# Unread products ahead of the two halves of the inverse's merge

## The chip, the cores and the metric

The kernel runs on one core of a Trainium2 chip. A core has a matrix engine (TensorE, PE in the profile), a vector engine (VectorE, DVE), a scalar engine (ScalarE, ACT), GpSimd (POOL) and SyncE (SP), which only issues DMAs. Each engine works through its own list of instructions in order, and waits at an instruction until what it needs from other engines is there. ACT issues DMAs too, and such an issue stands in its list like any other instruction. The metric is the device time of one execution, in microseconds (us).

## The reference, cut to what matters

One layer of a network for 128 prompt tokens and 512 latent tokens. It has a differential attention, a recurrent branch (RWKV7, run forward and backward), and a gated convolution. The change lies in the recurrent branch, which the reference writes as a scan over single tokens:

```python
def rwkv7_scan(s0, r, w, k, v, a, b, reverse):
    ...
    def step(S, inp):
        r_t, w_t, k_t, v_t, a_t, b_t = inp
        sa = jnp.einsum('bhvk,bhk->bhv', S, a_t)
        S = S * w_t[:, :, None, :] + sa[..., None] * b_t[:, :, None, :] + v_t[..., None] * k_t[:, :, None, :]
        return S, jnp.einsum('bhvk,bhk->bhv', S, r_t)
    s_final, ys = lax.scan(step, s0.astype(F32), xs, reverse=reverse)
    return jnp.moveaxis(ys, 0, 1), s_final
...
    q, k, v, rw, gates = jnp.split(proj, ...)      # proj = h @ p['w_in']
```

Eight heads of 64 channels run over 640 tokens in two directions. The other parts of the projection (queries, keys, values, gates) don't depend on the scan.

## The kernel before, in words

The scan is done in chunks of 64 tokens: 10 chunks, 2 directions, 4 pairs of heads. Inside a chunk the steps turn into a triangular system, whose 64x64 matrix must be inverted; between chunks a state of 64x64 is carried on. For each pair of heads i from 0 to 3 the main loop runs these stages:

- `rw_c` makes the triangular matrices of all 40 systems (2 heads, 2 directions, 10 chunks) in the tile MS.
- `rw_i` inverts the two 32x32 blocks on the diagonal of each, step by step on DVE (X, L711 and L713), turns one of them around into Y (L722) and puts the turned results back into MS (L725).
- `rw_m` merges: the block off the diagonal is a product of three 32x32 matrices. The first half (L735) multiplies 40 blocks of MS with Y into a PSUM bank `ps_m`, and ACT copies the result in four pieces to Vt (L737). The second half (L743) multiplies Vt with MS, into the other bank of the two, and DVE and ACT copy four pieces back to MS in turn (L745). Then the starting states are turned and scaled (L755 on PE, L756 on DVE into ST), the operands of the chain are turned (L766 on PE, L770 on ACT into AT), and the chain over the chunks runs: L781 solves, L802 and L805 join, L828 steps.
- `rw_e` and `rw_f` make the outputs, and `rw_b` prepares the next pair of heads (its square kk is L540, its norm rn L517 and L519).

TensorE would have little to do in these chains. So the main loop mixes in the big projections, which need nothing from the scan: `flow` is a generator over them, and `pull(n)` issues the next n products (L215, 128x128 times 128x320). There is a `pull(12)` between the halves of the merge. `pq` (L196) ties every product of this phase to the one before, so that TensorE keeps the order in which the program writes them.

The other engines keep no such order. The tile framework sorts the instructions of DVE, ACT, POOL and SP by its own estimate of when they can run. This matters at the second merge, where the query-key projection of one head ends nearby. There DVE scales a small bias (bs, L246), ACT evicts the product in three pieces to qkt (L956) and issues four DMAs that copy qkt with its 32-row blocks swapped to sw (L961). Then DVE multiplies qkt by the rotary table (L928, L929) while POOL does the same with sw, and DVE adds the two (L964). ACT splits off the high part (qkh, L223).

Of the kernel before, what the change touches and what calls it, by code (L numbers as in the profile page):

```python
# [18 lines left out]
P = 128  # L19
# [9 lines left out]
HALF = T // 2  # L29
# [37 lines left out]
def tile_layer(ctx, tc, x_prompt, x_sample, cache_k, cache_v, state_rwkv, c, c_ctx, w_ada, b_ada, w_in,  # L67
# [4 lines left out]
    nc = tc.nc  # L72
    def chain(prev, bi):
        if prev is not None:
            tc.add_manual_dep(bi.ins, prev.ins.name,
                              mybir.DependencyInfo(mybir.DependencyClass.NoSync, mybir.DependencyReason.DATA),
                              reason="psum group order")
        return bi
# [114 lines left out]
    def pq(bi):  # L193

        if order[0]:
            order[1] = chain(order[1], bi)  # L196
        return bi
# [60 lines left out]
    def bank(pool, tag, bufs=1):  # L258
        return pool.tile([P, 512], F32, name="ps_" + tag, tag=tag, bufs=bufs)
# [13 lines left out]
    xw, xa, xwl, xal = (cb.tile([P, T], F32R, name=n_) for n_ in ("xw", "xa", "xwl", "xal"))  # L273
# [4 lines left out]
    with tc.tile_pool(name="start", bufs=1) as sp, tc.tile_pool(name="psS", bufs=2, space=PSUM) as psS:  # L278
# [61 lines left out]
        for q in range(4):  # L340
# [4 lines left out]
            ps = psS.tile([P, 512], F32, name="ps_ada", tag="ada")  # L345
# [21 lines left out]
        ps, ps2 = (psS.tile([P, 512], F32, name="ps_ada", tag="ada") for _ in range(2))  # L367
# [5 lines left out]
        ps = psS.tile([P, 512], F32, name="ps_ada", tag="ada")  # L373
        prev = None
        for n, (s, w) in enumerate(((shh, wfh), (shh, wfl), (shl, wfh))):
            for kb in range(KB):
                prev = chain(prev, pq(nc.tensor.matmul(ps[0:32, :], s[:, kb, :], w[:, kb].rearrange("p b n -> p (b n)"),
                                                    start=n == 0 and kb == 0, stop=n == 2 and kb == KB - 1)))
        nc.scalar.copy(out=shb[0:32, :], in_=ps[0:32, :])
        ps = psS.tile([P, 512], F32, name="ps_ada", tag="ada")  # L380
# [24 lines left out]
    def token_shift(blk, out, pool, first=None, new=None):  # L405
        rt = raw[nraw[0] % 2]
        nraw[0] += 1

        def evac(cols, pd, bias):
            o = 1 if cols.start == 0 else 3  # L410
            nc.scalar.activation(out=rt[:, o + cols.start:o + cols.stop], in_=pd, func=AF.Identity, bias=bias)

        if first is None:
            yield from project_in(load_w(w_in[:, W_RW + blk * P:W_RW + (blk + 1) * P], KB), evac, new=new)
        elif first > 1:
            ps = firsts[first - 2]
            for v, cols, src in ((0, slice(0, TP), ps[0][:, 0:TP]), (1, slice(TP, HALF), ps[0][:, TP:HALF]), (1, slice(HALF, T), ps[1][:, 0:HALF])):
                evac(cols, src, bias0[:, first, v:v + 1])
        tmp = pool.tile([P, 650], F32, name="shtmp", tag="f", bufs=FB)[:, 0:642]
        nc.scalar.activation(out=tmp, in_=rt[:, 1:643], func=AF.Copy, scale=cmu[:, blk:blk + 1])  # L420
        m0, m1 = vec("mu0", blk), vec("mu1", blk)
        nc.vector.scalar_tensor_tensor(out=tmp, in0=rt[:, 0:642], scalar=m0, in1=tmp, op0=ALU.mult, op1=ALU.add)
        nc.vector.scalar_tensor_tensor(out=out[:, 0:TP], in0=rt[:, 2:130], scalar=m1, in1=tmp[:, 0:128], op0=ALU.mult, op1=ALU.add)
        nc.vector.scalar_tensor_tensor(out=out[:, TP:T], in0=rt[:, 132:644], scalar=m1, in1=tmp[:, 130:642], op0=ALU.mult, op1=ALU.add)
# [4 lines left out]
    def newx():  # L429

        nx[0] += 1
        return (lambda: psD.tile([P, 512], F32, name="ps_d")) if nx[0] % 2 == 0 else lambda: psX.tile([P, 512], F32, name="ps_x", tag="x")
# [8 lines left out]
    def pull(n):  # L441
        for _ in range(n):
            if next(flow[0], None) is None:
                while later:
                    later.pop(0)[1]()
                return False
            for x in later:
                x[0] -= 1
            while later and later[0][0] <= 0:
                later.pop(0)[1]()  # L450
        return True
# [19 lines left out]
    def ft(name, w=T):  # L471
        return rp.tile([P, 650], F32, name=name, tag="f", bufs=FB)[:, 0:w]
# [16 lines left out]

    R = [dict() for _ in range(4)]  # L490

    def rw_a(i):
        cs = slice(i * P, (i + 1) * P)
        upw = ft("upw", 2 * P).rearrange("p (d n) -> p d n", d=2)
        nc.sync.dma_start(out=upw[0:64], in_=rw_w_up[:, :, cs].rearrange("d k n -> k d n"))
        nc.sync.dma_start(out=upw[64:128], in_=rw_a_up[:, :, cs].rearrange("d k n -> k d n"))
        ups_ = rp.tile([P, 2, 2, P], F32R, name="ups", tag="ups", bufs=UPB)
        for z, o in ((0, 0), (1, 64)):
            here, there = slice(o, o + 64), slice(64 - o, 128 - o)
            nc.scalar.copy(out=ups_[here, z], in_=upw[here])  # L500
            nc.gpsimd.tensor_tensor(out=ups_[there, z], in0=upw[here], in1=ups_[here, z].bitcast(F32), op=ALU.subtract)
        r, kr = (rp.tile([P, T], F32, name=n_, tag="rk", bufs=2) for n_ in ("r", "kr"))
        v = rp.tile([P, T], F32, name="v", tag="v", bufs=2)
        R[i].update(r=r, kr=kr, v=v, upw=ups_)
        yield from token_shift(4 + i, kr, rp, 2 if i == 0 else None, None if i == 0 else newx())
        yield from token_shift(i, r, rp, 3 if i == 0 else None, None if i == 0 else newx())
        R[i].update(rk_in=1)
        yield from token_shift(8 + i, v, rp, None, newx())
        R[i].update(v_in=1)
# [218 lines left out]
    def rw_m(i):  # L728
        AR, BT, UV, gs, st_in, MS = (R[i][k] for k in ("AR", "BT", "UV", "gs", "st_in", "MS"))
        Y11 = R[i]["Y11"]  # L730
        Vt = rp.tile([64, 40, 32], F32, name="Vt", tag="bk", bufs=2)
        ps = bank(psR, "m", 2)
        for ix in range(40):
            g, sl = ix % 4, ix // 4
            pq(nc.tensor.matmul(ps[32 * g:32 * g + 32, sl * 32:sl * 32 + 32], MS[0:32, ix, 32:64], Y11[:, :, ix], start=True, stop=True))  # L735
# [2 lines left out]
                out=Vt[32:64, g::4, :], in_=ps[32 * g:32 * g + 32, 0:320].rearrange("p (c s) -> p c s", s=32))  # L738
        pull(12)
        ps = bank(psR, "m", 2)  # L740
        for ix in range(40):
            g, sl = ix % 4, ix // 4
            pq(nc.tensor.matmul(ps[32 * g:32 * g + 32, sl * 32:sl * 32 + 32], Vt[32:64, ix, :], MS[32:64, ix, 32:64], start=True, stop=True))  # L743
# [9 lines left out]
        ps = bank(psR, "m", 2)  # L753
# [250 lines left out]
    def gate(br, n):  # L1004
# [3 lines left out]
        def ev_g(cols, pd, bias):  # L1008
# [6 lines left out]
    vals, heads_, gates = ([lambda z=z: values(z) for z in range(4)], [lambda z=z: qk_head(z) for z in range(4)],  # L1015
                           [lambda z=z: gate(1 - z // 8, z % 8) for z in range(16)])
    pairs_ = [lambda i=i: rw_a(i) for i in range(4)]
    works = [pairs_[0]] + vals[0:3] + [pairs_[1], vals[3]] + heads_[0:2] + [pairs_[2]] + heads_[2:4] + gates[0:1] + [pairs_[3]] + gates[1:]
    flow[0] = (x for f in works for x in f())
# [5 lines left out]
    for i in range(4):  # L1025
        if i:
            rw_e(i - 1)
        else:
            pull(40)
        need(i, "v_in")  # L1030
        sides.append(rw_d(i))
        rw_c(i)
        if i:
            sides.append(rw_f(i - 1))
        rw_i(i)
        if i < 3:
            need(i + 1, "rk_in")
            sides.append(rw_b(i + 1))
        else:
            pull(10)  # L1040
        rw_m(i)
        while sides:
            side()
            pull(3)
# [17 lines left out]
    def abank(tag):  # L1062
        return psA.tile([P, 512], F32, name=tag, tag=tag)
# [14 lines left out]
    ps = abank("T")  # L1078
# [529 lines left out]
```

## Time and profile before

| | us |
|---|---|
| median of the runs shown (3) | 1409.14 |
| lowest and highest | 1409.0 and 1413.62 |
| the profiled execution | 1415.6 |
| its span, first to last instruction | 1413.6 |
| TensorE busy in the span | 1254.3 (89%) |
| DVE busy in the span | 960.7 (68%) |
| ACT busy in the span | 544.0 (38%) |

The profiled execution is one run of its own, and all durations below are from it. A row of the timeline has the start of a group of equal instructions, the time that it took from the first start to the last end, engine, line and operation. In brackets stands how long the engine had been idle, and what released it. The dense products overlap, so their distance and not their length tells the rate. The granted clock is shown as a share of full speed: 1.00 is 2.4 GHz and 0.50 is 1.2 GHz.

### The profile page before, as it was taken

What the parts mean: (1) busy time and instruction counts of PE and PEld (TensorE: products, weight loads), DVE (VectorE), ACT (ScalarE), POOL (GpSimd) and SP (SyncE); (2) the same over time, 40 slices, a digit from 0 to 9 for tenths busy, and PEclk for the clock granted to TensorE, in tenths of its full rate; (3) what the DMA queues carried; (4) which work ended last, traced back from release to release, by engine and by line L of the source; (5) the groups of instructions that cost most, each with busy time, mean ns of one, the idle gap of its engine ahead of it and who ended that gap; (6) DMA issues with size and microseconds to landing.
All of it is one profiled execution on the core that took longest, in us unless ns stands there. A gap on an engine that the chain in (4) does not pass through costs nothing. (4 is left out here: it accounts for less than half of the span.)

```text
span 1413.6 us, 26568 instructions
## 1 busy us (share of the span) xinstructions
PE 1254.3 (89%) x10583; PEld 1118.5 (79%) x10583; DVE 960.7 (68%) x1672; ACT 544.0 (38%) x1122; POOL 553.4 (39%) x415
## 2 busy tenths in 40 slices
PE   6989878887879899999888989969999999999995
PEld 5888777786768788889777777758988988989984
DVE  2367948896868667931366433687997987768778
ACT  3444333333333334232355321464443433434440
POOL 2244225432542232212220244546644635635631
PEclk9989979988998899989889999999999999999998
DMA  9412112221221111212666888423232231322222
GB/s 308 129 41 65 53 58 61 65 75 54 63 72 61 50 34 51 85 50 76 189 183 216 267 259 266 136 72 93 81 106 68 75 97 58 99 69 76 75 75 82
DMA packets 157455, 144.57 MB, mean 102 GB/s; under 512 B 10490, under 2 KB 128020, under 8 KB 157332
## 3 DMA queue, kind: packets, MB, share of 16 engines
q1 hardware_dynamic: 147490, 127.85, 29.6%
q10 hardware_dynamic: 9842, 15.03, 3.1%
q8 instruction: 83, 1.36, 0.4%
q14 instruction: 40, 0.33, 0.1%
HBM read 121.06 MB, written 19.69 MB: 100 GB/s over the span
## 5 line engine op out<-in xcount | busy, mean ns | idle before, releaser
L187 POOL TENSOR_TENSOR wl<-ws,wh 128x512 fp32r<-128x512 f32 x100 | 139.1, 1393 | 393.2 <-ACT wh L186 361.6
L224 POOL TENSOR_TENSOR wl<-sums,wh 128x512 fp32r<-128x512 f32 x88 | 137.0, 1562 | 39.4 <-ACT wh L223 35.7
L1431 PE MATMUL ps_d<-oph,wh 128*128 128x320 f32 x440 | 137.6, 313 | 11.6 <-DVE u L1443 5.2
L224 POOL TENSOR_TENSOR wl<-wu,wh 128x512 fp32r<-128x512 f32 x63 | 88.8, 1409 | 142.6 <-ACT wh L223 129.2
L1431 PE MATMUL ps_d<-oph,wl 128*128 128x320 f32 x440 | 137.0, 311 | 1.2 <-POOL wl L224 1.2
L1431 PE MATMUL ps_d<-opl,wh 128*128 128x320 f32 x440 | 136.5, 310 | 1.1 <-DVE opl L224 1.1
L186 ACT CAST wh<-ws 128x512 fp32r<-128x512 f32 x100 | 61.6, 618 | 136.7 <-PE ps_d L215 37.2
L215 PE MATMUL ps_d<-hh,wl 128*128 128x320 f32 (+1 forms) x304 | 102.8, 338 | 0.0
L215 PE MATMUL ps_x<-hh,wl 128*128 128x320 f32 (+1 forms) x304 | 101.6, 334 | 0.6 <-POOL wl L187 0.6
L215 PE MATMUL ps_d<-hl,wh 128*128 128x320 f32 (+1 forms) x304 | 102.0, 335 | 0.0
L215 PE MATMUL ps_x<-hh,wh 128*128 128x320 f32 (+1 forms) x304 | 101.8, 335 | 0.0
L215 PE MATMUL ps_d<-hh,wh 128*128 128x320 f32 (+1 forms) x304 | 101.6, 334 | 0.0
L215 PE MATMUL ps_x<-hl,wh 128*128 128x320 f32 (+1 forms) x304 | 101.2, 333 | 0.0
L1431 PEld LDWEIGHTS ps_d<-oph,wh 128*128 128x128 f32 x440 | 83.0, 189 | 16.0 <-ACT wh L223 9.1
L1431 PEld LDWEIGHTS ps_d<-opl,wh 128*128 128x128 f32 x440 | 83.0, 189 | 2.3 <-POOL hf L1346 1.3
L1431 PEld LDWEIGHTS ps_d<-oph,wl 128*128 128x128 f32 x440 | 83.1, 189 | 1.9 <-POOL wl L224 1.7
L223 ACT CAST wh<-sums 128x512 fp32r<-128x512 f32 x88 | 54.6, 620 | 64.7 <-PE ps_e L1431 25.2
L1465 PE MATMUL acc<-wh,gh 128*128 128x512 f32 x185 | 73.6, 398 | 2.6 <-ACT gh L223 2.6
L1466 PE MATMUL acc<-wl,gh 128*128 128x512 f32 x185 | 73.4, 397 | 0.0
L1467 PE MATMUL acc<-wh,gl 128*128 128x512 f32 x185 | 72.3, 397 | 0.5 <-DVE gl L224 0.5
L223 ACT CAST wh<-wu 128x512 fp32r<-128x512 f32 x63 | 39.1, 621 | 73.3 <-PE acc L1467 30.1
L215 PEld LDWEIGHTS ps_d<-hh,wl 128*128 128x128 f32 x304 | 61.9, 203 | 2.0
(430 smaller groups left out, 3649.7 us busy)
## 6 DMA issues: line engine op xcount, KB each, us to landing
wu<-in_w_up_dram SPq DMA_DIRECT2D x42, 512.0 KB
ws<-in_w_in_dram SPq DMA_DIRECT2D x76, 256.0 KB
wa<-in_w_ada_dram SPq DMA_DIRECT2D x24, 512.0 KB
ws<-in_w_down_dram SPq DMA_DIRECT2D x44, 256.0 KB
wa<-in_w_ada_dram SPq DMA_DIRECT2D x8, 1024.0 KB
ks<-qk_dram SPq DMA_DIRECT2D x32, 192.0 KB
g_dram<-tg ACTq DMA_DIRECT2D x16, 320.0 KB
tg<-g_dram SPq DMA_DIRECT2D x16, 320.0 KB
```

The costliest lines, as they stand in the source:

```text
L186: nc.scalar.copy(out=wh, in_=ws)
L187: (lo_eng or nc.gpsimd).tensor_tensor(out=wl, in0=ws, in1=wh.bitcast(F32), op=ALU.subtract)
L215: pq(nc.tensor.matmul(pd, w[:, k, :], x[:, g, sl], start=g == 0 and z == 0, stop=g == kb - 1 and z == 2))
L223: nc.scalar.copy(out=hi, in_=src)
L224: (lo_eng or nc.vector).tensor_tensor(out=lo, in0=src, in1=hi.bitcast(F32), op=ALU.subtract)
L1431: nc.tensor.matmul(ps, w[:, k, :], x[:, b, k, :], start=k == 0 and z == 0, stop=k == 3 and z == 2)
L1465: nc.tensor.matmul(acc, a_h, wh, start=first, stop=False)
L1466: nc.tensor.matmul(acc, a_h, wl, start=False, stop=False)
L1467: nc.tensor.matmul(acc, a_l, wh, start=False, stop=last)
```

## The change

A new helper writes n products of 128x128 times 128x320 into the first 320 columns of a given PSUM bank. Their operands are the tile xw, which stays in SBUF through this phase. Nobody reads the result: the products of the merge write the same columns afterwards, with `start=True`. The helper is called in `rw_m` ahead of the first half with 16 products for i = 1 and 2 (none for 0 and 3), and ahead of the second half with 10 products for all four i.

```diff
+    def unread(ps, n):
+
+        for _ in range(n):
+            pq(nc.tensor.matmul(ps[:, 0:HALF], xw[:, 0:P], xw[:, 0:HALF], start=True, stop=True))
...
         ps = bank(psR, "m", 2)
+        unread(ps, 16 if 0 < i < 3 else 0)
         for ix in range(40):
             g, sl = ix % 4, ix // 4
             pq(nc.tensor.matmul(ps[32 * g:32 * g + 32, sl * 32:sl * 32 + 32], MS[0:32, ix, 32:64], Y11[:, :, ix], start=True, stop=True))
...
         pull(12)
         ps = bank(psR, "m", 2)
+        unread(ps, 10)
         for ix in range(40):
```

The new lines shift the later ones: L735 and L737 become L741 and L743, L743 and L745 become L750 and L752, and all behind them (L756, L928, L956, L961, L964) get 7 more. L540 becomes L545.

The framework sorts the other engines' instructions anew around the added products. The first place is TensorE at the second merge (i = 1), from the end of the dense products ahead of it. Before:

```order
L215 MATMUL ps_x<-hl,wh 128x322
L215 MATMUL ps_x<-hh,wl 128x322
L215 MATMUL ps_x<-hh,wh 128x322
L735 MATMUL ps_m<-Y_3266,MS 32x32 x40
L215 MATMUL ps_x<-hl,wh 128x322
```

And now, where L495 is the helper's line:

```order
L215 MATMUL ps_x<-hl,wh 128x322
L215 MATMUL ps_x<-hh,wl 128x322
L215 MATMUL ps_x<-hh,wh 128x322
L495 MATMUL ps_m<-xw 128x320 x16
L741 MATMUL ps_m<-Y_3276,MS 32x32 x40
L215 MATMUL ps_x<-hl,wh 128x322
```

On TensorE nothing else has moved, here or elsewhere: the ten products of the second half stand between its dense products and L750 in the same way.

The second place is ACT at the same merge, from the two conversions of weights (wh) ahead of the Vt copies. Before:

```order
L186 CAST wh<-ws 128x512 x2
L737 COPY Vt<-ps_m 32x10x32 x4
L956 ACTIVATE qkt<-ps_d,bs 128x128
L956 ACTIVATE qkt<-ps_d,bs 128x192
L956 ACTIVATE qkt<-ps_d,bs 128x320
L961 DMA sw<-qkt 32x512 x4
L745 COPY MS<-ps_m 32x10x32
L770 COPY AT<-ps_m 64x512
L186 CAST wh<-ws 128x512
L745 COPY MS<-ps_m 32x10x32
```

And now:

```order
L186 CAST wh<-ws 128x512 x2
L963 ACTIVATE qkt<-ps_d,bs 128x128
L963 ACTIVATE qkt<-ps_d,bs 128x192
L963 ACTIVATE qkt<-ps_d,bs 128x320
L743 COPY Vt<-ps_m 32x10x32
L968 DMA sw<-qkt 32x512 x4
L743 COPY Vt<-ps_m 32x10x32 x3
L752 COPY MS<-ps_m 32x10x32 x2
L223 CAST qkh<-qkt 128x640
L1005 DMA qk_dram<-qkh 128x640
L777 COPY AT<-ps_m 64x512
```

The three evictions to qkt have moved ahead of all Vt copies, and the four DMA issues ahead of three of them. The conversion qkh and its DMA have moved ahead of the first copy to AT.

The third place is DVE at the same merge, from the small bias bs on. Before:

```order
L246 TENSOR_SCALAR bs<-ps_d 128x2
L745 COPY MS<-ps_m 32x10x32
L756 TENSOR_SCALAR ST<-ps_m,gs 128x64 x2
L745 COPY MS<-ps_m 32x10x32
L928 TENSOR_TENSOR qkt<-qkt,rope 128x512
L929 TENSOR_TENSOR qkt<-qkt,rope 128x512
L788 COPY QQ<-ps_ch 64x256
L964 TENSOR_TENSOR qkt<-qkt,sw 128x512
L517 TENSOR_SCALAR rn<-ps_m 128x10
```

And now:

```order
L246 TENSOR_SCALAR bs<-ps_d 128x2
L935 TENSOR_TENSOR qkt<-qkt,rope 128x512
L752 COPY MS<-ps_m 32x10x32
L936 TENSOR_TENSOR qkt<-qkt,rope 128x512
L752 COPY MS<-ps_m 32x10x32
L971 TENSOR_TENSOR qkt<-qkt,sw 128x512
L763 TENSOR_SCALAR ST<-ps_m,gs 128x64 x2
L795 COPY QQ<-ps_ch 64x256
L522 TENSOR_SCALAR rn<-ps_m 128x10
```

The three rotary instructions have moved ahead of the two scalings into ST, and the first of them ahead of the copies into MS. Elsewhere little has moved: at the third merge the square kk (L540) now stands ahead of ACT's four Vt copies instead of behind them, and DVE's bs there comes two instructions later. On POOL, at the second merge, the subtraction of one weight slab (L187) has moved behind the rotary work on sw. On SP two loads have changed places.

## Rows read from the trace of the kernel before

**Rows 1.** The table of waits, TensorE, 160 to 620 us: total, times, longest.

```profile
PE ps_m L743 <- ACT Vt L737: 8.4, 8, 2.4
```

**Rows 2.** Timeline of TensorE, second merge: start, us, instruction, idle time before.

```profile
320.37 0.44 PE L735 MATMUL ps_m<-Y,MS 32*32 32x32 f32 x16 [1.46 <-DVE Y L722]
324.19 1.23 PE L735 MATMUL ps_m<-Y,MS 32*32 32x32 f32 x64 [3.38 <-DVE Y L722]
...
332.25 0.63 PE L766 MATMUL ps_m<-ident,AR 128*64 128x128 f32 x4 [0.38 <-DVE ST L756]
...
341.72 0.33 PE L802 MATMUL ps_m<-BT,QQ 64*64 64x64 f32 x4 [0.65 <-DVE rn L517]
```

**Rows 3.** Timeline of ACT, second merge.

```profile
325.48 1.74 ACT L737 COPY Vt<-ps_m 32x320 f32<-32x320 f32 x4 [6.62 <-PE ps_m L735]
331.00 1.10 ACT L956 ACTIVATE qkt<-ps_d,bs 128x128 f32<-128x128 f32 x3 [3.78 <-DVE bs L246]
332.13 2.59 ACTq L961 DMA_DIRECT2D sw<-qkt  x4
```

**Rows 4.** Timeline of DVE, second merge.

```profile
330.81 0.15 DVE L246 TENSOR_SCALAR bs<-ps_d 128x2 f32<-128x2 f32 x1
330.88 0.47 DVE L745 COPY MS<-ps_m 32x320 f32<-32x320 f32 x1
331.28 0.26 DVE L756 TENSOR_SCALAR ST<-ps_m,gs 128x64 f32<-128x64 f32 x1
...
336.23 0.69 DVE L928 TENSOR_TENSOR qkt<-qkt,rope 128x512 f32<-128x512 f32 x1 [0.53 <-DMA sw<-qkt]
336.95 1.64 DVE L929 TENSOR_TENSOR qkt<-qkt,rope 128x512 f32<-128x512 f32 x1
...
340.89 0.69 DVE L964 TENSOR_TENSOR qkt<-qkt,sw 128x512 f32<-128x512 f32 x1 [1.85 <-POOL sw L929]
```

**Rows 5.** Timeline of TensorE, fourth merge.

```profile
600.10 0.32 PE L215 MATMUL ps_d<-hh,wl 128*128 128x322 f32 x1
600.25 0.31 PE L215 MATMUL ps_d<-hh,wh 128*128 128x322 f32 x1
602.93 2.60 PE L743 MATMUL ps_m<-MS,Vt 32*32 32x32 f32 x80 [2.37 <-ACT Vt L737]
...
607.17 1.06 PE L766 MATMUL ps_m<-ident,AR 128*64 128x128 f32 x4 [0.38 <-DVE ST L756]
...
608.30 0.47 PE L215 MATMUL ps_d<-hh,wl 128*128 128x322 f32 x1
608.56 0.47 PE L215 MATMUL ps_d<-hh,wh 128*128 128x322 f32 x1
```

**Rows 6.** Timeline of TensorE, first merge.

```profile
180.77 0.24 PE L743 MATMUL ps_m<-MS,Vt 32*32 32x32 f32 x2 [2.06 <-ACT Vt L737]
```

**Rows 7.** Timeline of TensorE, third merge.

```profile
479.92 1.27 PE L743 MATMUL ps_m<-MS,Vt 32*32 32x32 f32 x74 [0.20 <-ACT Vt L737]
...
482.70 1.06 PE L766 MATMUL ps_m<-ident,AR 128*64 128x128 f32 x4 [0.38 <-DVE ST L756]
...
491.28 0.33 PE L802 MATMUL ps_m<-BT,QQ 64*64 64x64 f32 x4
```

**Rows 8.** Timeline of POOL, second merge.

```profile
336.38 1.67 POOL L187 TENSOR_TENSOR wl<-ws,wh 128x512 fp32r<-128x512 f32 x1 [16.17 <-ACT wh L186]
338.01 1.49 POOL L928 TENSOR_TENSOR sw<-sw,rope 128x512 f32<-128x512 f32 x1
339.58 1.28 POOL L929 TENSOR_TENSOR sw<-sw,rope 128x512 f32<-128x512 f32 x1
```

**Rows 9.** Timeline of ACT, third merge.

```profile
478.12 1.74 ACT L737 COPY Vt<-ps_m 32x320 f32<-32x320 f32 x4
...
480.46 0.82 ACT L540 ACTIVATE kk<-kr,vT 128x640 f32<-128x640 f32 x1
```

**Rows 10.** Table by stretch: us, busy per engine, granted clock, DMA share, GB/s.

```profile
602.70:612.90 10.20, 8.60 (x122) 7.11 (x124) 1.69 (x5) 4.14 (x10) 1.54 (x2) 0.50 0.27 85
```

## The prediction

> **What bounds the kernel now.** I read the table of waits first, for TensorE in 160 to 620 us, because that stretch holds the four merges. Its longest entry is the merge's second half waiting for the copies of Vt: 8.4 us over eight waits [rows 1]. The view lists ACT, DVE and a little POOL as releasers and no DMA. So in this stretch TensorE and the two vector engines hand work to each other, and a delay of one handover moves all that follows. I call the merges by their order: first near 180 us, second near 325, third near 475, fourth near 600. Then I read the timelines, engine by engine, around the second merge. TensorE stands idle 1.46 us before the first 16 rows of the first half, and 3.38 us before the rest, both times for a DVE transpose [rows 2]. ACT makes four Vt copies as soon as the first half is done, and only then takes up the query-key block: three evictions at 331.00 (1.10 us) and four DMA issues (2.59 us) [rows 3]. DVE is busy without a break up to the small copy bs at 330.81, and bs is what those evictions wait for [rows 4].
>
> **The change part by part.** It adds 72 products of 128x320: 10 in front of the second half in all four merges, 16 in front of the first half in the second and third. It removes nothing. They wait for nothing. One costs 0.15 us, the distance between two such products at full clock, or 0.26 at half clock [rows 5].
>
> *The products themselves.* The 16 take 16 x 0.15 = 2.4 us and start where the idle time starts, at 320.37 - 1.46 = 318.9. They end near 321.3, so the first sixteen small products begin 0.9 us late, but the other 64 wait until 324.19 anyway [rows 2]. Cost 0. The ten take 1.5 us. They fit into 2.06 us of waiting in the first merge [rows 6] and 2.37 in the fourth [rows 5]. Cost 0. If this cover were gone, they would cost 72 x 0.15 = 10.8 us in all.
>
> *The moved instructions, second merge.* The order shows more than an insertion. ACT now has the three evictions and the four DMA issues around the Vt copies: evictions, one copy, four DMA issues, three copies. And DVE has the rotary work of the query block (L928, L929, L964) between the copies into MS and ahead of the two scalings L756 that start the state chain. I follow this with durations of before, on the clock of before:
> - bs ends at 330.96 and the evictions start at 331.00 as now, since nothing ahead of them moves. They end at 332.1 [rows 3, 4].
> - One Vt copy (1.74 / 4 = 0.43) to 332.5. Four DMA issues, 2.59, to 335.1. Three copies, 1.31, to 336.4 [rows 3].
> - The second half needs all four copies. Its last 74 products took 1.27 us at half clock [rows 7], and after such a wait I take that: done at 337.7.
> - DVE: L928 waits for the four transfers. It began at 336.23, which is 1.5 us after the last issue ended (334.72) [rows 3, 4], so now at 336.6. It ends at 337.3, before the products, and costs nothing. The first MS copy (0.47) ends at 338.2 [rows 4].
> - L929 took 1.64 us, and L928 of the same shape 0.69 [rows 4]. Then the second MS copy, 0.48, and L964, 0.69, which also waits for POOL's two multiplications: 336.6 + 1.49 + 1.28 = 339.4 [rows 8]. So L964 ends at 340.1 with the short L929 and at 341.1 with the long one. I take 341.1, because POOL's L929 runs through just that time.
> - L756 begins at 341.2 instead of 331.28, 9.9 us late (8.9 with the short L929) [rows 4].
>
> On L929 the trace and a page can be weighed. Its 1.64 us fell together with a POOL subtraction at 336.38 of 1.67 us [rows 8]. The Trainium skill, "SBUF — State Buffer", section "SBUF: two separate sides", says that VectorE with two operands in SBUF and GpSimd hold their shared ports one at a time, each for its whole instruction. By that rule L929 could stand behind both multiplications of POOL, and L964 would end at 339.4 + 0.69 + 0.48 + 0.69 = 341.3 rather than 341.1. The rows agree in that L929 was long only under a POOL instruction, and the sum would grow by 0.2 us.
>
> Behind L756 wait the second transpose L755, the transposes L766 and with them the whole state chain, since TensorE works in order. Something comes back: from L766 (332.25) to the first L802 (341.72) before took 9.47 us, with 0.65 of waiting at its end for rn, which stood behind L964 [rows 2, 4]. That rotary work is done earlier now. The third merge, where it isn't in the way, takes 482.70 to 491.28 = 8.58 us [rows 7]. So 9.9 - 0.9 = 9.0 us late at L802. Bounds: 8.9 - 0.9 = 8.0, and 9.9 if nothing comes back.
>
> *The moved instruction, third merge.* The square L540 (0.82 us) now stands ahead of the four Vt copies [rows 9]. They begin 0.8 us later. The copies, not the products, are what ends the wait there. Against this stands a possible return of the clock (next term). I take +0.5, bounds +0.8 and -1.2 (0.8 - 2.0).
>
> *The clock.* In the fourth merge the granted clock is 0.50, that is 1.2 GHz, from 602.70 to 612.90 [rows 10], after TensorE had waited from 600.6 to 602.9 [rows 5]. With 1.5 us of that wait filled it may stay at 2.4 GHz. Worth: two groups of transposes L766, 1.06 against 0.63 us each [rows 2, 5], and ten dense products, 10 x (0.26 - 0.15) = 1.1, together 2.0 us. The second half itself gains next to nothing: it is paced by the copies. I take -1.5, bounds 0 and -2.0. First merge: after the ten products TensorE still waits, and what follows the copies hangs on DVE. I take 0, bounds 0 and -2.0.
>
> **Sum.** 0 + 9.0 + 0.5 - 1.5 = +8.0 us. Against its own time, 1415.6 us for the profiled execution (a span of 1413.6 and 2.0 around it), this is 1423.6. The median of the runs shown is 1409.14, 6.5 lower; I carry the difference over: 1409.1 + 8.0 = 1417.1 us. Nothing later takes the delay up, as far as I can see, because DVE and ACT wait with TensorE and what they do next is fed by it.
>
> **The rivals.**
> - *The clock pays most of it back.* The stall costs its 9.0, the square 0.8, but the other three merges each return 2.0: +3.8, 1412.9 us. For it: the clock does fall at these places, and the fill goes just where it is lost. Against: in the first and third merge the wait for the copies ends with more waiting after the fill.
> - *The delay is taken up.* The stretch after the second merge has long DVE work. If that had slack the 9 us would vanish, leaving 0.5 - 1.5 = -1.0, 1408.1 us. For it: TensorE waits for DVE again later. Against: DVE idles through the same stall, so its later work starts later too.
> - *Faster.* The Vt copies keep their time, because the evictions find bs early or the DMA issues pass quickly, and all four merges run at 2.4 GHz from the second half through the second L766: 4 x 2.0 - 0.8 = 7.2 us gained, 1401.9 us. It decides if the copies of the second merge end before 331 us of the old scale. The Trainium skill, "TensorE: Matmul & The Clock Gate", section "Why this matters for your kernels", speaks for this: idle gaps between bursts bring the array back to half clock, so filling them should pay. By that rule alone the time would be the 1401.9 of this rival. The clock in the fourth merge agrees with it; the place of bs on DVE speaks against the rest [rows 4].
> - *The products land on the path.* If the order shifts the waits so that half or more of the 72 have no wait to hide in, 5 to 11 us come on top of the stall: 1422 to 1428 us. Against: each has a wait in front that is longer.
>
> **How the numbers follow.** A difference below 0.5% (7.0 us) can't be told from no change here. Chances: forecast 0.57, with own bounds from 8.0 + 0.5 - 2.0 = +6.5 to 9.9 + 0.8 = +10.7; clock pays back 0.17; taken up 0.12; faster 0.05; on the path 0.09. Four fifths of the forecast's own range lies above 7.0, so slower is 0.57 x 0.8 + 0.09 = 0.55, same 0.11 + 0.17 + 0.12 = 0.40, faster 0.05. The range runs from 1410 (most of the rival in which the clock pays) to 1421 (the forecast's upper bound and a little), and leaves out the faster case, most of "taken up" and most of the last.
>
> **What would show it.** In the second merge: ACT with evictions before the first Vt copy and the four issues before the other three; Vt done some 9 us later than before; TensorE idle twice, before the second half and again before the second L755; L964 ahead of L756 on DVE; the distance from the last transpose Y to the first L802 longer by about 9 us. In the third: L540 before Vt. In the fourth: granted clock 1.00 up to L766 or beyond. I am wrong if the Vt copies of the second merge end less than 5 us later than before, or if that distance grows by less than 6 us.

## The result and the profile after

The changed kernel took 1420.12 us (median of 4 runs, 1419.58 to 1420.44) against 1409.12 for the kernel before (4 runs, 1409.0 to 1413.62). The ratio is 1.0078, with a 95% interval from 1.005 to 1.0107: 11.0 us slower, 7 to 15. The forecast was 1417.1. The profiled execution took 1419.58 with a span of 1417.6; that of before took 1415.6, so these two profiles differ by only 4.0 us.

The table of waits of the changed kernel, TensorE, 160 to 620 us:

```profile
PE ps_m L750 <- ACT Vt L743: 10.3, 14, 2.3
...
PE ps_m L762 <- DVE ST L763: 4.9, 4, 3.0
```

The wait for Vt has grown although ten products now stand in front of it in every merge [rows 1], and a wait for ST with 3.0 us in one piece is new. Both are at the second merge. TensorE there:

```profile
318.03 1.21 PE L741 MATMUL ps_m<-Y,MS 32*32 32x32 f32 x64 [2.71 <-DVE Y L727]
...
326.47 0.24 PE L750 MATMUL ps_m<-MS,Vt 32*32 32x32 f32 x2 [2.25 <-ACT Vt L743]
328.96 2.15 PE L750 MATMUL ps_m<-MS,Vt 32*32 32x32 f32 x78 [2.24 <-ACT Vt L743]
...
334.45 0.37 PE L762 MATMUL ps_m<-ident,st_in 64*128 64x64 f32 x1 [3.04 <-DVE ST L763]
334.75 1.06 PE L773 MATMUL ps_m<-ident,AR 128*64 128x128 f32 x4
...
344.10 0.33 PE L809 MATMUL ps_m<-BT,QQ 64*64 64x64 f32 x4
```

Against [rows 2] there are three waits between the halves and the transposes L773, and the transposes run at half clock: 1.06 us against 0.63, with a granted clock of 0.50 from 334.75 to 339.30. ACT, second merge:

```profile
324.88 1.09 ACT L963 ACTIVATE qkt<-ps_d,bs 128x128 f32<-128x128 f32 x3 [12.32 <-DVE bs L246]
326.00 0.41 ACT L743 COPY Vt<-ps_m 32x320 f32<-32x320 f32 x1
326.01 2.44 ACTq L968 DMA_DIRECT2D sw<-qkt  x4
328.49 1.30 ACT L743 COPY Vt<-ps_m 32x320 f32<-32x320 f32 x3 [2.07 <-DMA sw<-qkt]
```

ACT has been idle for 12.32 us when bs comes, because the evictions at the head of its list wait for it. The result of the first half lies ready for the last 5.6 of these (318.03 + 1.21 to 324.88); before, ACT copied it in that time [rows 3]. DVE, and then POOL, second merge:

```profile
324.70 0.15 DVE L246 TENSOR_SCALAR bs<-ps_d 128x2 f32<-128x2 f32 x1
330.01 0.69 DVE L935 TENSOR_TENSOR qkt<-qkt,rope 128x512 f32<-128x512 f32 x1 [5.16 <-DMA sw<-qkt]
331.15 0.48 DVE L752 COPY MS<-ps_m 32x320 f32<-32x320 f32 x1 [0.45 <-PE ps_m L750]
331.56 0.67 DVE L936 TENSOR_TENSOR qkt<-qkt,rope 128x512 f32<-128x512 f32 x1
...
333.39 0.69 DVE L971 TENSOR_TENSOR qkt<-qkt,sw 128x512 f32<-128x512 f32 x1 [0.64 <-POOL sw L936]
334.11 0.28 DVE L763 TENSOR_SCALAR ST<-ps_m,gs 128x64 f32<-128x64 f32 x1
```

```profile
330.05 1.55 POOL L935 TENSOR_TENSOR sw<-sw,rope 128x512 f32<-128x512 f32 x1 [16.11 <-DMA sw<-qkt]
331.68 1.67 POOL L936 TENSOR_TENSOR sw<-sw,rope 128x512 f32<-128x512 f32 x1
```

From bs to the first scaling L763 it is 9.41 us, against 0.47 before [rows 4]: 8.94 late. The first BT,QQ product comes 19.40 us after bs, against 10.91 [rows 2, 4]: 8.49 late. The copies of Vt end 5.1 us after bs, where before they ended 3.6 ahead of it, so the forecast's own test (at least 5 us later) is met.

For all further comparisons I use one distance, read from the one profiled execution of each kernel: from the end of the last transpose Y of a merge to the start of its first BT,QQ product. Before it was 19.2, 17.6, 19.1 and 23.1 us in the four merges; after, 19.5, 26.1, 19.1 and 22.7. So the second merge lost 8.5 us and the other three together nothing that counts.

### The profile page after: what moved, and what is told of

The parts are those of the page before. It is cut to its first block, busy times and chain, and to the rows that moved or that the text cites. A ratio compares the mean times of both kernels' runs of the same rounds, so it can differ in the third digit from the quotient of the medians.

```text
span 1417.6 us, 26713 instructions
## 1 busy us (share of the span) xinstructions
PE 1262.4 (89%) x10655; PEld 1126.3 (79%) x10655; DVE 957.4 (68%) x1672; ACT 543.5 (38%) x1122; POOL 553.3 (39%) x415
## 5 line engine op out<-in xcount | busy, mean ns | idle before, releaser
L187 POOL TENSOR_TENSOR wl<-ws,wh 128x512 fp32r<-128x512 f32 x100 | 138.7, 1389 | 379.6 <-ACT wh L186 352.9
L224 POOL TENSOR_TENSOR wl<-sums,wh 128x512 fp32r<-128x512 f32 x88 | 136.8, 1560 | 38.6 <-ACT wh L223 35.1
L223 ACT CAST wh<-sums 128x512 fp32r<-128x512 f32 x88 | 54.6, 620 | 64.4 <-PE ps_e L1438 25.3
L215 PEld LDWEIGHTS ps_d<-hh,wh 128*128 128x128 f32 x304 | 61.6, 203 | 1.5 <-issue 0.2
```

Of the source, the lines that this page charges most:

```text
L187: (lo_eng or nc.gpsimd).tensor_tensor(out=wl, in0=ws, in1=wh.bitcast(F32), op=ALU.subtract)
L215: pq(nc.tensor.matmul(pd, w[:, k, :], x[:, g, sl], start=g == 0 and z == 0, stop=g == kb - 1 and z == 2))
L223: nc.scalar.copy(out=hi, in_=src)
L224: (lo_eng or nc.vector).tensor_tensor(out=lo, in0=src, in1=hi.bitcast(F32), op=ALU.subtract)
```

## The experiments

Where an experiment holds an order, it gives the framework a pair of instructions of one engine; `behind([later], earlier)` (names shortened here) fixes their order and adds no wait. `vt`, `ms` and `st` are the merge's copies to Vt, to MS and its two scalings (st[2] is DVE's first copy to QQ); `ev`, `dma`, `rot` and `add` are the evictions, DMA issues, rotary multiplications and addition of the query-key block; `at` are the copies to AT, `ar` is DVE's first addition into AR, `square` is the square kk.

### The products or the order

All 72 products, with the order of before held on ACT and DVE (old_order):

```diff
+        if i == 1:
+            behind(ev, vt[3])
+            behind([rot[0]], st[1])
+            behind([add], st[2])
+        if i == 2:
+            behind([square], vt[3])
```

> All 72 unread products stay where the change has them; the order of ACT and DVE is held as before the change at the second and third merge (Vt copies ahead of the evictions and DMA issues, scalings into ST ahead of the rotary work, square kk behind the Vt copies). Theory (the moved instructions cost the time): the loss of 11.0 us goes; what stays is the clock's small return, 0 to 3 us faster than before, 1406 to 1409 us. Rival (the products themselves lie on the path): still 8 us or more slower, 1417 us or more. If both share, 1412 to 1416.

No product, but the second merge's order as in the changed kernel (order_alone):

```diff
+        if i == 1:
+            behind([vt[0]], ev[2])
+            behind([dma[0]], vt[0])
+            behind([vt[1]], dma[3])
+            behind([ms[0]], rot[0])
+            behind([ms[2]], rot[1])
+            behind([st[0]], add)
```

> No unread product at all; only the order of ACT and DVE at the second merge is made that of the changed kernel. Theory: most of the loss comes without any product, 8 to 11 us slower than before, 1417 to 1420 us. Rival (products on the path, or the two only together): within 2 us of before, 1407 to 1411 us.

The first took 1408.16 us, ratio 0.9991 [0.9962, 1.0019], distance 17.3 us. The second took 1417.87, ratio 1.0062 [1.0036, 1.0089], distance 26.2. With the products the loss goes when the order goes; without a product it is there when the order is. DVE with the order alone:

```profile
333.69 0.69 DVE L950 TENSOR_TENSOR qkt<-qkt,rope 128x512 f32<-128x512 f32 x1 [5.17 <-DMA sw<-qkt]
...
337.06 0.69 DVE L988 TENSOR_TENSOR qkt<-qkt,sw 128x512 f32<-128x512 f32 x1 [0.64 <-POOL sw L951]
337.79 0.28 DVE L775 TENSOR_SCALAR ST<-ps_m,gs 128x64 f32<-128x64 f32 x1
```

The two waits, 5.17 and 0.64, are those of the changed kernel to 0.01 us. And TensorE and DVE with all products in the old order:

```profile
331.38 0.89 PE L768 MATMUL ps_m<-MS,Vt 32*32 32x32 f32 x80
```

```profile
332.31 0.48 DVE L770 COPY MS<-ps_m 32x320 f32<-32x320 f32 x1 [0.16 <-PE ps_m L768]
```

Here the ten products have no wait for Vt to hide in, and the second half starts later. But DVE, busy up to bs, waits only 0.16 us for it.

### Which products turn the order

Only the sixteen (only16), and only the tens (only10):

```diff
-        unread(ps, 10)
+        unread(ps, 0)
```

> Only the 16 products ahead of the first half of the second and third merge; none ahead of any second half. The order of the other engines is that of the changed kernel word for word. Theory: as slow as the changed kernel or a little slower, 1419 to 1422 us, since the ten are free and give back little. Rival (each product costs its 0.15 us): 40 of 72 products gone, 6 us less than the changed kernel, 1414 us.

```diff
-        unread(ps, 16 if 0 < i < 3 else 0)
+        unread(ps, 0)
```

> Only the ten products ahead of the second half of each merge; none ahead of the first half. The order of ACT and DVE ahead of the Vt copies is that of before. Theory: no stall at the second merge, 0 to 3 us faster than before, 1406 to 1409 us. Rival (products on the path): 40 x 0.15 = 6 us slower, 1415 us.

The sixteen alone give the new order and the loss of the second merge: 1417.12 us, ratio 1.006 [1.0036, 1.0084], distance 26.0. By its middle that is a little under the 1419 to 1422 expected, and nearer to them than to the rival's 1414. The tens keep the old order ahead of Vt; they took 1413.23, ratio 1.0027 [1.0005, 1.0048], distance 18.2, slower than the 1406 to 1409 expected. In that version the framework has put the first copy to QQ behind the addition:

```profile
341.33 0.69 DVE L971 TENSOR_TENSOR qkt<-qkt,sw 128x512 f32<-128x512 f32 x1 [2.42 <-POOL sw L936]
342.05 0.42 DVE L795 COPY QQ<-ps_ch 64x256 f32<-64x256 f32 x1
```

That explains 0.6 us of its 3.8. The tens were run again with the order held as in old_order (ten_pinned):

> The kernel before with the ten products ahead of each second half and none of the sixteen, and with the order of ACT and DVE at the second merge held as before. Theory: the ten products cost nothing, and the 0.27% of the version with the tens alone came from the order that the framework chose there (the addition to qkt ahead of the copy to QQ) or from scatter: ratio 0.998 to 1.001, 17.0 to 17.8 us from the last transpose Y to the first BT,QQ product of the second merge. Rival: the ten products themselves cost some 3 to 4 us somewhere; then the ratio is 1.002 to 1.003 with the old order too.

1408.86 us, ratio 1.0003 [0.9979, 1.0027], distance 17.7. The products ahead of the second half cost nothing that can be measured, within some 3 us either way. The rest of only10's 3.8 us stays unexplained; its interval reaches down to 0.7 us. In its profile another 2.8 us lie behind the first BT,QQ product of the second merge (59.6 us from there to the next AR,BK product, against 56.9), but two executions of the changed kernel differ by 2.2 there.

### Which engine's order

Only ACT's new order (act_alone), and only DVE's (dve_alone), each without a product:

```diff
+            behind([vt[0]], ev[2])
+            behind([dma[0]], vt[0])
+            behind([vt[1]], dma[3])
+            behind([rot[0]], st[1])
+            behind([rot[0]], ms[2])
+            behind([add], st[2])
```

> The kernel before, without any added product. Only ACT's list at the second merge is put as in the changed kernel (three evictions, one Vt copy, four DMA issues, three Vt copies); DVE's list stays as before. Theory: ACT's and DVE's new orders are two delays beside each other, not one after the other. With ACT's alone the copies into MS begin some 6.4 us late, the first scaling into ST too, and up to 2.7 us come back because the copy to AT no longer stands behind the DMA issues: from the last transpose Y to the first BT,QQ product 17.6 + 3.5 to 6 = 21 to 24 us, ratio 1.0025 to 1.0045. Rival: ACT's order is the whole cause, and the distance is 26 us (ratio 1.006). Second rival: DVE's order is the whole cause, and it is 17 to 18 us (ratio 1.000).

```diff
+            behind(ev, vt[3])
+            behind([ms[0]], rot[0])
+            behind([ms[2]], rot[1])
+            behind([st[0]], add)
```

> The kernel before, without any added product. Only DVE's list at the second merge is put as in the changed kernel (rotary multiplications around the copies into MS, the addition ahead of the scalings into ST); on ACT all Vt copies stay ahead of the evictions. Theory of two delays beside each other: the first rotary multiplication waits for the four transfers as before (5.4 us after bs) and the copies into MS and the scalings now wait behind it, so the first scaling comes some 9 us late with nothing late on ACT: 25 to 26.5 us from the last transpose Y to the first BT,QQ product, ratio 1.005 to 1.0065. Rival, the delays add up: 2 to 3 us, 19.6 to 20.6 us, ratio 1.002. Rival, ACT's order is the whole cause: 17 to 18 us, ratio 1.000.

ACT's order alone: 1419.12 us, ratio 1.0059 [1.0028, 1.009], distance 23.7. DVE's alone: 1416.68, ratio 1.0053 [1.0029, 1.0078], distance 26.1. By its middle the first lies above the 1.0025 to 1.0045 expected, and the times can't tell the two apart. The distances can: they are 6.1 and 8.5 us longer, and both orders together 8.5. So these are two delays beside each other. DVE and TensorE with DVE's order alone:

```profile
336.81 0.69 DVE L948 TENSOR_TENSOR qkt<-qkt,rope 128x512 f32<-128x512 f32 x1 [5.17 <-DMA sw<-qkt]
...
340.11 0.69 DVE L986 TENSOR_TENSOR qkt<-qkt,sw 128x512 f32<-128x512 f32 x1 [0.64 <-POOL sw L949]
340.83 0.28 DVE L773 TENSOR_SCALAR ST<-ps_m,gs 128x64 f32<-128x64 f32 x1
```

```profile
341.17 0.36 PE L772 MATMUL ps_m<-ident,st_in 64*128 64x64 f32 x1 [10.21 <-DVE ST L773]
```

Vt and the second half are as early as before, and TensorE still waits 10.21 us, for a scaling that stands behind the query block on DVE. With ACT's order alone, DVE waits for the second half instead, and scales at once:

```profile
336.49 0.48 DVE L764 COPY MS<-ps_m 32x320 f32<-32x320 f32 x1 [6.30 <-PE ps_m L762]
336.90 0.26 DVE L775 TENSOR_SCALAR ST<-ps_m,gs 128x64 f32<-128x64 f32 x1
```

### The changed kernel beside these

The changed kernel was run once more on the same chip as ten_pinned, act_alone and dve_alone (after_again).

> The changed kernel once more, beside the others. If the second merge is the whole of the change, 8.5 us, it stands level with the two kernels that have the new order with no or fewer products (ratios 1.0062 and 1.0060): 1.005 to 1.007. If the products cost something of their own besides, it stays at the 1.0078 of the first comparison or above, 2 to 3 us over those.

1421.99 us, ratio 1.0083 [1.0044, 1.0122], distance 25.3: the same result, and the upper of the two expected cases by its middle. Whether the products, together with the new order, cost 2 to 3 us that the order without them does not is open: the intervals of 1.0083 and 1.0062 overlap in most of their length, and with the old order the same 72 products gave 0.9991.

### Products without cover

The version ten_pinned with 40 products in place of 10 ahead of each second half (forty):

```diff
-        unread(ps, 10)
+        unread(ps, 40)
```

> As the version with ten products ahead of each second half and the old order held, but with 40 instead of 10. That version leaves TensorE idle between its tens and the last 74 products of the second half for about 3.1 us (first merge), 0 (second), 1.8 (third) and 2.2 us (fourth), counted from the end of the tens to the start of those 74 less the few products between. Thirty more take 30 x 0.15 = 4.5 us. Theory (a product is free up to the wait behind it and costs its whole time beyond): +1.1, +4.5, +2.9 and +2.3 = 10.8 us at the ends of the second halves, 0 to 3 of it given back by the clock: +8 to +11 us, ratio 1.0055 to 1.008; from the last transpose Y to the first BT,QQ product 20.5, 22, 21 and 24.5 us. Rival: the clock, held at 2.4 GHz into the chain, pays for most of it: below +5 us, ratio below 1.0035.

1413.76 us, ratio 1.0025 [0.9998, 1.0053]. The distances are 19.8, 20.0, 19.5 and 23.7 us, together 4.9 longer than with ten, where I expected 10. The rival was nearer. TensorE in the second merge, and the table by stretch from 325.0 to 338.5 us (busy per engine, granted clock, DMA share, GB/s):

```profile
325.15 6.33 PE L495 MATMUL ps_m<-xw 128*128 128x320 f32 x40
331.40 0.89 PE L768 MATMUL ps_m<-MS,Vt 32*32 32x32 f32 x80
...
333.71 0.63 PE L791 MATMUL ps_m<-ident,AR 128*64 128x128 f32 x4 [0.38 <-DVE ST L781]
```

```profile
325.00:338.50 13.50, 12.55 (x185) 11.74 (x184) 6.67 (x11) 4.30 (x11) 3.96 (x3) 0.97 0.11 26
```

The second half starts 4.2 us later than with ten, near the 4.5 expected. But the clock then stays at 2.4 GHz through both groups of transposes (0.63 and 0.60 us, against 0.99 and 0.64 with ten) and the dense products between them, and the first BT,QQ product is only 2.2 us late. From the first group to the second it is 1.9 us here and 3.5 with ten, so 1.5 of the 2.0 us that came back are the clock's; most of the rest is a wait for rn, 0.39 us with ten, that is gone. Over the four merges the second halves end 9.8 us later than with ten, and the distances are 4.9 longer: about half of what the uncovered products cost came back. Both groups kept the full clock at the second and third merge alone; at the first the second group took 1.06 us.

### Holding the query block back further

Two candidates to beat both kernels. The order of before with the block held behind the start of the chain (chain_first), and all 72 products with the same hold, the evictions held behind Vt and the square behind the third merge's Vt (fill_chain):

```diff
+            behind(dma, ms[3])
+            behind(dma, at[1])
+            behind([rot[0]], st[2])
+            behind([add], ar)
```

> The kernel before, without any added product. At the second merge the query-key block is held back further than before: its four DMA issues behind ACT's copies into MS and the second copy to AT, its rotary multiplications behind DVE's first copy to QQ, its addition behind the first addition into AR. Theory: in the kernel before, the copy to MS waits 2.66 us for the DMA issues, the second group of transposes 0.53 us for the copy to AT, and the first BT,QQ product 0.65 us for a small instruction of DVE behind the addition. These last two, 1.2 us, go: 16.4 us from the last transpose Y to the first BT,QQ product instead of 17.6, ratio 0.999, which the times can't tell from no change. Rival: the rotary work only moves into the chain behind it, and the stretch from that product to the next stage grows by 1 us or more: ratio 1.000 or above.

> All 72 products of the change, with the query-key block of the second merge held back as in the version named chain_first, and the square ahead of the third merge's copies of Vt held behind them as before the change. It is the candidate to beat both. Theory: the products cost nothing and bring back some clock in the third and fourth merge (1.1 us in all in the version with all products and the old order), the held block another 1.2: ratio 0.997 to 0.9995. Rival: neither reaches the end of the kernel, or the scatter hides it: 0.9985 to 1.0015.

The first took 1410.01 us, ratio 1.0014 [0.9986, 1.0041]; the second 1421.1, ratio 1.0081 [1.0055, 1.0108]. The distances of the second merge are 16.4 us, as expected, and 16.8, but the rival of chain_first holds: from the first BT,QQ product to the next AR,BK product it took 60.3 us against 56.9, because the block now stands in the way a group later. The time of fill_chain lies above both of its expected ranges. ACT and TensorE with fill_chain, at the second group:

```profile
345.99 0.72 ACT L223 CAST qkh<-qkt 128x640 fp32r<-128x640 f32 x1 [1.31 <-DVE qkt L997]
...
347.81 0.37 ACT L815 COPY QQ<-ps_ch 64x256 f32<-64x256 f32 x1
```

```profile
348.23 0.27 PE L831 MATMUL ps_m<-BT,QQ 64*64 64x64 f32 x1 [1.17 <-ACT QQ L815]
```

From the last Y to the third group's BT,QQ products it is 30.4 us in the kernel before and 35.1 and 35.7 here. From Y to the next AR,BK product it is 74.4 before, 76.7 with chain_first and 81.1 with fill_chain. So 6.6 us of what fill_chain lost (11.4 by the ratio) lie in this stretch; where the rest lies isn't shown. None of the versions is measurably faster than the kernel before. Best of those with products is the old order held.

## Why the prediction was right

**The place and the chain.** The second merge was named as the place and the order as the cause; old_order, order_alone and only16 show both. The forecast +8.0 lies inside the measured 7 to 15. That its terms add up to so near the 8.4 us of the four distances is in part luck: 9.0, 0.5 and -1.5 were forecast for the second, third and fourth merge, and 8.5, 0.0 and -0.4 came, with 0.3 in the first; errors of either sign cancel. The range was also narrower than its terms: with the lower bounds given for the first and third merge its low end is 8.0 - 1.2 - 2.0 - 2.0 = +2.8 and not +6.5, and of 6.5 to 10.7 the share above 7.0 is 0.88, not four fifths.

**Second merge, +9.0 forecast, 8.5 measured.** The scaling was 8.94 us late, not 9.9. I had given DVE's second multiplication 1.64 us, as it took under POOL's subtraction [rows 4, 8]. It took 0.67, and POOL's two took 1.55 and 1.67, so that POOL set the start of the addition. That the sum with the short multiplication comes out right (8.9) is a second stroke of luck: the four DMA issues did not stand behind the Vt copy but began beside it, and the first multiplication started 5.3 us after bs instead of 5.8, while POOL's two together took 0.5 us longer than I had given them. In the version with ACT's order alone DVE was idle at the first of them and had only work from PSUM at the second. POOL there:

```profile
335.38 1.04 POOL L950 TENSOR_TENSOR sw<-sw,rope 128x512 f32<-128x512 f32 x1 [15.93 <-DMA sw<-qkt]
336.50 1.26 POOL L951 TENSOR_TENSOR sw<-sw,rope 128x512 f32<-128x512 f32 x1
```

So meeting DVE cost POOL 0.51 and 0.41 us. In each meeting the one that began first kept its time: DVE by 0.04 and 0.12 us in the changed kernel, POOL by 0.57 us in the kernel before. The Trainium skill, "SBUF — State Buffer", section "SBUF: two separate sides", says just this of a VectorE instruction with two operands in SBUF and a GpSimd instruction that reads SBUF: whichever starts first holds the shared ports for the whole instruction. The rows agree on who waits, though POOL lost a little less than the 0.65 and 0.55 us that were left of DVE's instructions; my use of the page had the two the wrong way round.

**What comes back, 0.9 forecast, 0.45 measured.** The wait for rn did go (0.65 in [rows 2]). But after the long waits both groups of transposes ran at half clock, 1.06 us each against 0.63 and 0.91 before.

**A step that was wrong in its reason.** I wrote of DVE's first rotary multiplication that it ends before the products "and costs nothing", and counted the delay through ACT, Vt and the products. The delay through DVE alone is as long. It was in my sum, but as the tail of ACT's delay; dve_alone shows that it needs no late Vt.

**The products, 0 forecast.** Shown by old_order and ten_pinned, to within some 3 to 5 us of the time. The price without cover, each its full 0.15 us, was about twice too high: in forty the second halves ended 9.8 us later and the distances grew by 4.9.

**Third merge, +0.5 forecast, 0.0 measured.** ACT and TensorE of the changed kernel there:

```profile
482.19 0.81 ACT L545 ACTIVATE kk<-kr,vT 128x640 f32<-128x640 f32 x1
483.03 1.74 ACT L743 COPY Vt<-ps_m 32x320 f32<-32x320 f32 x4
```

```profile
483.50 0.24 PE L750 MATMUL ps_m<-MS,Vt 32*32 32x32 f32 x2 [1.17 <-ACT Vt L743]
...
484.82 0.84 PE L750 MATMUL ps_m<-MS,Vt 32*32 32x32 f32 x74 [0.20 <-ACT Vt L743]
```

The square costs its 0.8, and the last 74 products took 0.84 us in place of 1.27 [rows 7]; the two groups of transposes took 0.96 and 0.67 in place of 1.06 and 0.81. The two parts show singly: with the square ahead and no tens the distance was 19.7 us (only16), with the tens and the square held behind 18.3 (ten_pinned) and 16.8 (old_order), against 19.1. Here the return of the clock is the tens' doing: all five kernels with ten products there have 0.84 us for those 74, and of the six with none five have 1.27 and one (chain_first) 0.98.

**Fourth merge, -1.5 forecast, -0.4 measured.** The table by stretch of the changed kernel:

```profile
604.70:609.40 4.70, 3.21 (x92) 2.59 (x90) 0.08 (x2) 3.90 (x9) 1.35 (x2) 1.00 0.35 112
609.40:616.40 7.00, 5.93 (x44) 4.95 (x36) 1.69 (x5) 2.09 (x5) 1.18 (x1) 0.55 0.17 49
```

The granted clock was 2.4 GHz through the second half, against 1.2 GHz in [rows 10], and the 80 products took 2.17 us in place of 2.60 [rows 5]: that is the whole 0.4, and I had given it next to nothing. But the fill need not be its cause. The kernel only16 has no product in this merge and TensorE the same wait:

```profile
609.56 0.24 PE L750 MATMUL ps_m<-MS,Vt 32*32 32x32 f32 x2 [2.37 <-ACT Vt L743]
```

```profile
606.95:611.65 4.70, 1.73 (x82) 1.12 (x80) 0.08 (x2) 3.90 (x9) 1.35 (x2) 1.00 0.33 106
```

There too the granted clock is 1.00, and the distance is 22.7 us. So it is in order_alone and dve_alone (22.7) and chain_first (22.4), while act_alone is as before (23.2). After this wait, unfilled in all six (2.37 us, 2.70 in chain_first), the clock fell in two of these executions and not in four, so the 0.4 can't be put down to the products. What I had counted on, both groups of transposes and the dense products between them at 2.4 GHz, did not come: the clock fell to 1.2 GHz before the transposes, and both groups took 1.06 us as before [rows 5]. This term was mis-sized by at least 1.1 us, the most of all.

**The rivals.** "The delay is taken up" falls: from the first BT,QQ product of the second merge to the next AR,BK product it is 56.9 us before and 58.3 and 56.1 in two executions of the changed kernel, so nothing near 9 us is taken up. "The clock pays most back" falls too: the first, third and fourth distance together are 0.1 us shorter, and 0.4 in the second profile of the changed kernel, not 6. "Faster" falls by its own condition: the copies of Vt end 5.1 us after bs, which is 335.9 on the old scale and not before 331. "The products land on the path" falls by old_order, where all 72 are there and the interval of the ratio ends at 1.0019. What lies between the 8.4 us of the four distances and the measured 11.0 is within the interval. Without the second merge's distance, the spans of the profiled executions lie between 1387.7 and 1396.9 us in all kernels but fill_chain, and the two of the changed kernel are 1391.5 and 1388.9. A stretch without change, from one `rw_c` to the transposes Y, took 73.8 us in one of them and 69.1 in the other.

## What to carry to other kernels

Where a framework sorts the engines that you don't order by hand, an added instruction on one engine is a change to all: read the new order of the others before you price the instruction. When two lists have been reordered, try each alone, since two delays beside each other make a sum that fits either story; here undoing one would have left 6.1 or 8.5 us. And a block that stands in the way can be moved too far: held behind one handover, it stood in front of the next. Where a clock differs between two single executions, find out what it does in kernels without the change before the change gets the credit.

## What the runs showed of the hardware

Thirty more products ahead of each second half put its end back by 9.8 us in all and the first BT,QQ product by half of that; at the second and third merge TensorE then kept 2.4 GHz through the transposes behind them. Ten products kept it through the second half at the third merge (0.84 us for the last 74 products against 1.27) and not surely through the first group of transposes (0.62 to 0.96 us). At the fourth merge TensorE idled 2.37 us with no fill, and the clock behind it was 1.00 in only16 and 0.50 in the kernel before. Four DMA issues on ACT took 2.44 us in the changed kernel, and a copy behind them waited 2.07; in fill_chain the four took 3.52.
